# Dilated attention on one core: the product of the probabilities with V, its two exact halves in one matmul and its two heads in two banks

## The chip, the cores and the metric

The kernel runs on one core of a Trainium2 chip, as one launch. The metric is the device time of an execution in microseconds (us). TensorE (PE in the profile) multiplies matrices and writes to PSUM, which has eight banks of 512 float32 columns in each of 128 partitions. PEld is TensorE's loading of weights, which overlaps its matmuls. VectorE (DVE), ScalarE (ACT) and GpSimd (POOL) work beside it. DMAs are issued here from the queue of SyncE (SP) and of ScalarE.

## What is computed

A decoder trunk of two layers over 1024 positions of width 1024. The first layer mixes positions by a gated MLP, the second by attention; each is followed by a dense MLP with squared ReLU. The change lies in the attention. It has 8 heads of width 64 and three groups, each with its own queries, keys and values: dilations 1, 4 and 16, with windows of 128, 512 and 2048 positions. In each, a query attends to up to 129 keys, one dilation apart. Cut to what matters:

```python
def _dilated_group(q, k, v, bias_table, window, dilation):
    ...
    s = jnp.einsum('bnqrhc,bnkrhc->bnrhqk', qb, kc) * (HEAD_DIM ** -0.5)
    ...
    logits = jnp.where(valid[None, :, None, None], s + bias[None, None, None], NEG_INF)
    m = jnp.max(logits, axis=-1)
    p = jnp.exp(logits - m[..., None])
    den = jnp.sum(p, axis=-1)
    num = jnp.einsum('bnrhqk,bnkrhc->bnqrhc', p, vc)
    ...

def _dilated_attention_mixer(h, w_qkv, w_out, rel_bias):
    ...
    m_all = jnp.max(jnp.stack(maxs), axis=0)
    scales = [jnp.exp(m_ - m_all) for m_ in maxs]
    num_sum = sum(n_ * c[..., None] for n_, c in zip(nums, scales))
    den_sum = sum(d_ * c for d_, c in zip(dens, scales))
    o = (num_sum / den_sum[..., None]).astype(h.dtype).reshape(B_, S_, ATT_WIDTH)
    return o @ w_out
```

The line that the change touches is `num`, the product of the probabilities p with the values.

## The kernel before

Everything is kept transposed: channels on partitions, positions along the free axis. Products are made with more than one pass: `split` (lines 207 to 209) writes a float32 array as a rounded half `hi` (ScalarE's copy, L208) and the rest `lo` (VectorE's subtraction, L209). A dense product is three matmuls, hi by hi, hi by lo and lo by hi.

The attention is worked in 12 units: four pairs of heads (`hp`), and for each pair the three groups in the order dilation 4, 16, 1 (`ORDER`, `g` = 1, 2, 0). A unit has four blocks `j` of 256 queries, in two parts of 128. A block passes through three steps:

- `scores` (L1086): twelve matmuls give the scores of both heads, in two banks; VectorE adds the bias and takes the row's extreme (L1105), ScalarE takes the exponential and its sum (L1107). The tiles of probabilities are called `t`.
- `turned` (L1111): TensorE transposes each head's probabilities in blocks of 128 by 128 (L187, two to four blocks a head), and `split` makes the halves `ph` and `pl`, tiles `tr` (in the last unit `p`), with one instruction on ScalarE (L208) and one on VectorE (L209) for each head.
- `values` (L1124): V lies in SBUF as hi and lo of both heads side by side, so that a stationary block of 128 columns is hi and lo of one head. Each block of keys is multiplied with `ph` and then with `pl` into the same columns of one bank `pv`, which holds both heads (256 queries each). A block of keys that both parts of the queries see takes 256 columns, others 128. Then for each head ScalarE copies the product with V's lo half to `N` (L1144) and VectorE adds the product with V's hi half (L1145).

When all three groups of a pair are there, `merge` weights and adds their `N`, and `project` multiplies the result by the output matrix and adds it to the residual `h` (L306).

PSUM is shared out in two pools: three banks `mm` for the projections of q and k and of the output (`mm_bank`), five banks `at` for the attention's steps (`at_bank`). A tile gets a bank when an earlier one has been read out.

The order on TensorE is written by the planner `Flow`: the main stream multiplies q and k of the next unit (24 matmuls of 512 columns per half, 8 groups of three), and between those groups of three the generators of the attention are resumed when the planned time (`LAT`) of what they wait for has passed. The other engines' order is chosen by a scheduler; `tc.high_priority` puts a few steps ahead. Each engine works through its queue in order. At a unit's last block, `exchange` (L1216) sends the statistics through memory (`sc`, `ex`), on SP's queue, on which the loads of the next bias rows (`bvec`, L906 and L911) stand too; a bias tile is turned round by VectorE at L916.

## Time and profile before

| what | value |
|---|---|
| median of three runs | 2191.18 us (2187.42, 2191.18, 2191.38) |
| the profiled execution | 2188.09 us, span 2186.4 us |
| mean granted clock of TensorE in it | 0.995 |
| TensorE busy | 2142.4 us, 98% of the span |
| VectorE, ScalarE, GpSimd busy | 71%, 50%, 24% |
| stretch of the attention's blocks | about 1065 to 1520 us of the span |

A row of the timeline gives the start, the time that it covers, the engine, the line and operation, output and inputs (without buffer numbers), shape and count; in brackets stands the idle time before it and what ended it. A matmul's duration overlaps the next one's, so the pace of a run of matmuls is read from the starts. A row of a group has the count, then busy us and mean ns of one, then idle time before and what ended it. A row of the waits has who waited for whom: us in total, how often, the longest.

### The profile page before, as it was taken

The page shows a single profiled execution, that of the slowest core. Times are in us where ns is not written, and L with a number is a line of the kernel's source. Part 1 is how long each engine was busy: PE and PEld are TensorE (multiplying, and loading weights), DVE is VectorE, ACT ScalarE, POOL GpSimd, SP SyncE. Part 2 cuts the span into 40 slices and gives each one's busy share as a digit, 9 for nine tenths or more (in the row PEclk, how much of TensorE's full clock was granted, in tenths as well). Part 3 has the DMA queues.
Part 4 walks back from the last instruction along what each step waited for, and adds up shares of the span by engine and source line. Part 5 has one row for each costly group of instructions (what it writes and reads, how often), then busy time and mean ns, then how long its engine had stood idle before and what let it go on. Part 6 is the DMA issues. An engine that isn't in the chain of part 4 may idle for free.

```text
span 2186.4 us, 30394 instructions
## 1 busy us (share of the span) xinstructions
PE 2142.4 (98%) x10360; PEld 1776.8 (81%) x10360; DVE 1551.1 (71%) x2855; ACT 1087.4 (50%) x2200; POOL 515.5 (24%) x372
## 2 busy tenths in 40 slices
PE   8999999999999999999999999999999999999997
PEld 7888887888878888788888887887778888788886
DVE  7875268766689887771357676658986667988867
ACT  7644135555564444351355564656555556544433
POOL 2000124333323333510000000001443332332335
PEclk9999999999999999999999999999999999999999
DMA  6321104444355443333322222221154443644422
GB/s 222 110 75 49 48 22 150 165 150 152 132 172 172 151 155 117 109 113 138 121 68 62 74 65 54 75 55 30 39 179 157 149 152 121 195 161 150 150 90 99
DMA packets 167679, 253.88 MB, mean 116 GB/s; under 512 B 33641, under 2 KB 59364, under 8 KB 167524
## 3 DMA queue, kind: packets, MB, share of 16 engines
q1 hardware_dynamic: 166768, 250.71, 35.7%
q8 instruction: 81, 1.33, 0.3%
q10 hardware_dynamic: 756, 1.23, 0.2%
q14 instruction: 74, 0.61, 0.1%
HBM read 182.50 MB, written 69.37 MB: 115 GB/s over the span
## 4 chain that ended last, share of the span: by engine, by line
PE 77%; DVE 10%; DMA 6%; ACT 4%; issue 2%; POOL 1%; SPq 1%; DVEq 0%; ACTq 0%; POOLq 0%
PE at L180 38%; PE mm L180 37%; PE at L187 1%; DVE wp L209 1%; ACT t L1107 1%; DMA t<-bvec 1%; DMA h<-in_xT 1%; DMA t<-hid 1%; DMA t<-in_w_dl 1%; DVE y L209 1%; DMA sc<-st 1%; DVE h L797 1%; DVE N L1145 1%; DMA hr<-hid 1%; DVE hx L209 1%
## 5 line engine op out<-in xcount | busy, mean ns | idle before, releaser
L208 ACT ACTIVATE wp<-r 128x512 fp32r<-128x512 f32 (+2 forms) x404 | 240.6, 600 | 359.1 <-PE at L180 240.3
L180 PE MATMUL at<-hx,wp 128*128 128x512 f32 x1770 | 413.1, 389 | 3.7 <-DVE h L797 3.7
L180 PE MATMUL mm<-y,whi 128*128 128x512 f32 x1312 | 412.3, 395 | 0.0
L180 PEld LDWEIGHTS at<-hx,wp 128*128 128x128 f32 x1770 | 332.0, 188 | 73.8 <-DVE h L797 4.5
L209 DVE TENSOR_TENSOR wp<-r,wp 128x512 fp32r<-128x512 f32 (+2 forms) x404 | 319.9, 801 | 66.0 <-ACT wp L208 62.3
L180 PE MATMUL at<-t,wp 128*128 128x512 f32 x1344 | 313.9, 389 | 0.1
L180 PEld LDWEIGHTS at<-t,wp 128*128 128x128 f32 x1344 | 252.2, 188 | 52.8 <-DVE t L713 0.5
L262 POOL TENSOR_TENSOR t<-t 128x512 f32<-128x512 f32 (+1 forms) x66 | 82.8, 1255 | 866.2 <-ACT t L257 864.1
L180 PEld LDWEIGHTS mm<-y,whi 128*128 128x128 f32 x1312 | 240.7, 188 | 50.6
L180 PE MATMUL mm<-y,wlo 128*128 128x512 f32 x656 | 255.9, 390 | 0.0
L180 PE MATMUL mm<-y,wp 128*128 128x512 f32 x912 | 224.3, 392 | 5.3 <-ACT t L694 4.8
L349 POOL TENSOR_TENSOR t<-r 128x512 f32<-128x512 f32 (+3 forms) x62 | 90.4, 1457 | 579.4 <-DMA r<-in_w_dn 164.2
L180 PEld LDWEIGHTS mm<-y,wp 128*128 128x128 f32 x912 | 171.5, 189 | 43.4 <-ACT t L694 5.7
L180 PE MATMUL mm<-hx,wp 128*128 128x512 f32 x708 | 172.4, 390 | 2.5 <-DVE hx L209 1.3
L180 PEld LDWEIGHTS mm<-hx,wp 128*128 128x128 f32 x708 | 132.6, 188 | 31.5 <-DVE hx L209 2.3
L209 DVE TENSOR_TENSOR hx<-t,hx 128x512 fp32r<-128x512 f32 x192 | 146.6, 770 | 1.8 <-ACT hx L208 1.8
L180 PEld LDWEIGHTS mm<-y,wlo 128*128 128x128 f32 x656 | 123.1, 188 | 26.6
L797 DVE TENSOR_TENSOR h<-h,at 128x512 f32<-128x512 f32 x144 | 97.6, 682 | 48.2 <-PE at L180 46.4
L209 DVE TENSOR_TENSOR wlo<-r,whi 128x512 fp32r<-128x512 f32 x138 | 97.6, 725 | 46.4 <-ACT whi L208 42.0
L208 ACT ACTIVATE hx<-t 128x512 fp32r<-128x512 f32 x192 | 119.0, 630 | 18.1 <-DMA t<-hid 11.7
L208 ACT ACTIVATE whi<-r 128x512 fp32r<-128x512 f32 x138 | 84.0, 627 | 88.3 <-PE mm L180 56.9
L180 PE MATMUL at<-y,wp 128*128 128x512 f32 x480 | 119.0, 390 | 0.7 <-DVE wp L209 0.7
(199 smaller groups left out, 3214.0 us busy)
## 6 DMA issues: line engine op xcount, KB each, us to landing
t<-hid SPq DMA_DIRECT2D x182, 256.0 KB, 3.5
hid<-t SPq DMA_DIRECT2D x140, 256.0 KB, 2.3
r<-in_w_up SPq DMA_DIRECT2D x128, 256.0 KB, 2.7
r<-in_w_dn SPq DMA_DIRECT2D x88, 256.0 KB, 2.6
hid<-b SPq DMA_DIRECT2D x56, 256.0 KB, 2.1
r<-in_w_qkv SPq DMA_DIRECT2D x50, 256.0 KB, 2.6
r<-in_w_v SPq DMA_DIRECT2D x48, 256.0 KB, 3.5
vd<-vs SPq DMA_DIRECT2D x16, 512.0 KB, 3.9
```

Of the source, the lines that this page charges most:

```text
L180: nc.tensor.matmul(out, lhsT, rhs, **kw)
L187: nc.tensor.transpose(out, src, ident)
L208: nc.scalar.activation(hi, src, AF.Copy)
L209: nc.vector.tensor_tensor(lo, src, hi.bitcast(F32), op=ALU.subtract)
L262: nc.gpsimd.tensor_tensor(self.acc, self.acc, sq, op=ALU.add)
L349: tt(r3, r[0, 0], r[1, 0], op=ALU.subtract)
L797: engine.tensor_tensor(hs[i, s], hs[i, s], src, op=ALU.add)
L1107: nc.scalar.activation(p[:, c], p[:, c], AF.Exp, bias=m, scale=-1.0, accum_out=dn)
L1145: nc.vector.tensor_tensor(o, o, pv[r, c], op=ALU.add)
```

## The change

`turned` splits the probabilities so that the halves of a part of the queries lie in one tile, hi first, lo behind: a tile [128, 2, columns] for each part and head, instead of one tile for each half. The number of tiles stays; for a head there are now two instructions on ScalarE and two on VectorE instead of one and one, each over that part's columns. In the last unit one tile still takes both parts, and one `split` does it.

`values` multiplies a block of V with both halves at once: the moving operand is [128, 2, 128], and the product goes to [128, 2, 128] of the bank, hi's product in its first 256 columns and lo's in its last 256. So a head needs a bank of its own: head 0 takes one from `at`, head 1 one from `mm`. ScalarE copies V's lo product with the probabilities' hi half; VectorE adds the hi product, and then, with an instruction more, V's hi product with the probabilities' lo half. The product of the two lo halves, which the kernel before took in, is left out. The planner counts as many columns as before, so the places of the steps on TensorE stay.

```diff
     def turned(u, j, ps, last=False):
-        _, _, width = geometry(u.g, j)
+        keys, at, width = geometry(u.g, j)
         out = []
         for p in ps:
             pt = at_bank()
             for b in range(width // P):
                 transpose(pt[:, blk(b)], p[:, blk(b)])
-            ph, pl = pair("p").both() if last else (rtemp(), rtemp())
-            with tc.high_priority(offset=PRIO):
-                split(ph[:, :width], pl[:, :width], pt[:, :width])
-            out.append((ph, pl))
+            if last:
+                x = slot((P, 2, HALF), F32R, "p")
+                with tc.high_priority(offset=PRIO):
+                    split(x[:, 0, :width], x[:, 1, :width], pt[:, :width])
+                pp = [x[:, :, at[i]:at[i] + keys[i][1] * P] for i in range(2)]
+            else:
+                pp = []
+                for i in range(2):
+                    x, w = rtemp().rearrange("p (e k) -> p e k", e=2), keys[i][1] * P
+                    with tc.high_priority(offset=PRIO):
+                        split(x[:, 0, :w], x[:, 1, :w], pt[:, at[i]:at[i] + w])
+                    pp.append(x)
+            out.append(pp)
         return out
 
     def values(u, j, pts):
         keys, at, _ = geometry(u.g, j)
-
-        parts = {}
-        for i in range(2):
-            for x in range(keys[i][1]):
-                parts.setdefault(keys[i][0] + x, []).append((at[i] + x * P, i * P))
-        pv = at_bank()
         for hd in range(2):
-            lst = list(parts.items())
-            for n, (kb, cs) in enumerate(lst):
-                pc, oc, w = cs[0][0], hd * 2 * P + cs[0][1], len(cs) * P
-                tv, at_ = place(u.g, kb)
-                va = u.V[tv][:, at_, 2 * hd:2 * hd + 2, :]
-                for e in range(2):
-                    matmul(pv[:, oc:oc + w], va, pts[hd][e][:, pc:pc + w], start=(hd == 0 and n == 0 and e == 0),
-                           stop=(n == len(lst) - 1 and e == 1), skip_group_check=True)
-        for hd in range(2):
+
+            pv = mm_bank() if hd else at_bank()
+            p3 = pv.rearrange("p (e q) -> p e q", e=2)
+            for i in range(2):
+                for x in range(keys[i][1]):
+                    tv, at_ = place(u.g, keys[i][0] + x)
+                    matmul(p3[:, :, blk(i)], u.V[tv][:, at_, 2 * hd:2 * hd + 2, :], pts[hd][i][:, :, blk(x)],
+                           start=(i == 0 and x == 0), stop=(x == keys[i][1] - 1), skip_group_check=True)
             r, x = slice(64 * hd, 64 * hd + 64), slice(64 - 64 * hd, 128 - 64 * hd)
-            o, c = u.N[r, 2 * j * P:(2 * j + 2) * P], slice(hd * 2 * P, (hd + 1) * 2 * P)
-            nc.scalar.activation(o, pv[x, c], AF.Copy)
-            nc.vector.tensor_tensor(o, o, pv[r, c], op=ALU.add)
+            o = u.N[r, 2 * j * P:(2 * j + 2) * P]
+            nc.scalar.activation(o, p3[x, 0], AF.Copy)
+            nc.vector.tensor_tensor(o, o, p3[r, 0], op=ALU.add)
+            nc.vector.tensor_tensor(o, o, p3[r, 1], op=ALU.add)
```

On TensorE the change replaces the rows of each call of `values` and leaves the others where they were. This is the first call, block 0 of the first unit (dilation 4), between the products of the main stream and the next transposes (`at` and `mm` are the pool of the output's bank, `tr` the halves):

```order
 L180 MATMUL mm<-y,whi 128x512 x2
 L180 MATMUL mm<-y,wlo 128x512
-L180 MATMUL at<-tr,V 128x256 x2
-L180 MATMUL at<-tr,V 128x128 x2
-L180 MATMUL at<-tr,V 128x256 x2
-L180 MATMUL at<-tr,V 128x128 x2
+L180 MATMUL at<-tr,V 128x2x128 x3
+L180 MATMUL mm<-tr,V 128x2x128 x3
 L187 MATMUL at<-ident,t 128x128 x6
```

Eight matmuls into one bank have become three into a bank of `at` and three into a bank of `mm`.

On VectorE, this is the place in the second pair's unit of dilation 4 at which block 0's product is read out, while the first pair is projected. Before, `at_10810` is the bank of both heads and `mm_10766` holds a half of the next unit's k:

```order
L1145 TENSOR_TENSOR N_10809<-N_10809,at_10810 64x256
L1062 SCALAR_TENSOR_TENSOR k1_10941<-mm_10766,k0_10940 128x32x16
L209 TENSOR_TENSOR tr_10828<-at_10823,tr_10827 128x384
L209 TENSOR_TENSOR tr_10836<-at_10831,tr_10835 128x384
L1145 TENSOR_TENSOR N_10809<-N_10809,at_10810 64x256
L1105 ISA t_10853,st1_10570<-at_10839,b_10100 128x128
```

The same place after it, where `at_10860` holds head 0's product and `mm_10867` head 1's, and `mm_10816` is that half of k:

```order
L1147 TENSOR_TENSOR N_10859<-N_10859,at_10860 64x256
L1062 SCALAR_TENSOR_TENSOR k1_11001<-mm_10816,k0_11000 128x32x16
L209 TENSOR_TENSOR tr_10878<-at_10874,tr_10878 128x128
L1148 TENSOR_TENSOR N_10859<-N_10859,at_10860 64x256
L1147 TENSOR_TENSOR N_10859<-N_10859,mm_10867 64x256
L209 TENSOR_TENSOR tr_10881<-at_10874,tr_10881 128x256
L209 TENSOR_TENSOR tr_10888<-at_10884,tr_10888 128x128
L1148 TENSOR_TENSOR N_10859<-N_10859,mm_10867 64x256
L1105 ISA t_10908,st1_10616<-at_10894,b_10133 128x128
```

Between the reading of k and the first scores stand three subtractions and three adds where two and one stood; a fourth subtraction follows behind the first scores.

On TensorE again, this is where that unit's last block is multiplied, in front of the next unit's first projection. Before (`mm_10944` is the second half of k, `mm_11032` an output projection, `mm_11053` the next unit's q):

```order
L180 MATMUL mm_10944<-y_8580,wlo_10756 128x512
L180 MATMUL at_11013<-tr_10979,V_10595 128x256
L180 MATMUL at_11013<-tr_10980,V_10595 128x256
L180 MATMUL at_11013<-tr_10979,V_10596 128x128
L180 MATMUL at_11013<-tr_10980,V_10596 128x128
L180 MATMUL at_11013<-tr_10987,V_10595 128x256
L180 MATMUL at_11013<-tr_10988,V_10595 128x256
L180 MATMUL at_11013<-tr_10987,V_10596 128x128
L180 MATMUL at_11013<-tr_10988,V_10596 128x128
L180 MATMUL mm_11032<-o_10806,whi_10693 128x512 x2
L180 MATMUL mm_11032<-o_10806,wlo_10692 128x512
L180 MATMUL mm_11053<-y_8347,whi_11044 128x512 x2
```

After it, with `mm_11004`, `mm_11098` and `mm_11119` in their places:

```order
L180 MATMUL mm_11004<-y_8580,wlo_10806 128x512
L180 MATMUL at_11078<-tr_11040,V_10641 128x2x128
L180 MATMUL at_11078<-tr_11043,V_10641 128x2x128
L180 MATMUL at_11078<-tr_11043,V_10642 128x2x128
L180 MATMUL mm_11085<-tr_11050,V_10641 128x2x128
L180 MATMUL mm_11085<-tr_11053,V_10641 128x2x128
L180 MATMUL mm_11085<-tr_11053,V_10642 128x2x128
L180 MATMUL mm_11098<-o_10856,whi_10743 128x512 x2
L180 MATMUL mm_11098<-o_10856,wlo_10742 128x512
L180 MATMUL mm_11119<-y_8347,whi_11110 128x512 x2
```

Between the second half of k and the next q there were one `mm` tile, and are now two.

## The prediction

> **What bounds the kernel now.** I read the page first, then the busy time by stretches, the groups of instructions by shape, the waits of the attention stretch, and the timelines of TensorE and VectorE around single products.
>
> ```profile
> span 2186.4 us, 30394 instructions
> ...
> PE 2142.4 (98%) x10360; PEld 1776.8 (81%) x10360; DVE 1551.1 (71%) x2855; ACT 1087.4 (50%) x2200; POOL 515.5 (24%) x372
> ```
>
> ```profile
> core 0: us, PE busy (x) PEld busy (x) DVE busy (x) ACT busy (x) POOL busy (x), PEclk, DMA share, GB/s
> 1065.00:1520.00 455.00, 446.90 (x2698) 371.31 (x2698) 297.05 (x888) 258.88 (x726) 2.14 (x2) 1.00 0.23 64
> ...
> 1490.00:1525.00 35.00, 32.05 (x185) 27.11 (x186) 31.82 (x74) 22.23 (x53) 6.49 (x5) 0.95 0.09 31
> ```
>
> TensorE is busy 98% of the span, and 446.90 of the 455 us in which the attention runs, at a granted clock of 1.00. VectorE has 297.05 us there (65%). So a matmul less is worth its time, as long as nothing makes TensorE wait afterwards. Only in the last 35 us is VectorE as full as TensorE (31.82 of 35.00).
>
> **What the matmuls cost.** The change touches 48 calls of `values`: 16 each for the three dilations. In a timeline row, the time of a run of matmuls is the distance from its start to the next row's start.
>
> ```profile
> L180 PE MATMUL at<-tr,V 128*128 128x128 f32 x276 | 40.0, 260 | 0.0
> ...
> L180 PE MATMUL at<-tr,V 128*128 128x256 f32 x112 | 24.2, 298 | 0.0
> ```
>
> ```profile
> 1097.46 1.04 PE L180 MATMUL at<-tr,V 128*128 128x256 f32 x8
> 1098.33 0.84 PE L187 MATMUL at<-ident,t 128*128 128x128 f32 x6
> ...
> 1129.49 1.01 PE L180 MATMUL at<-tr,V 128*128 128x128 f32 x8
> 1130.34 0.62 PE L187 MATMUL at<-ident,t 128*128 128x128 f32 x4
> ...
> 1505.99 2.93 PE L180 MATMUL at<-p,V 128*128 128x128 f32 x24
> 1508.75 0.63 PE L187 MATMUL at<-ident,t 128*128 128x128 f32 x4
> ...
> 2162.68 3.48 PE L180 MATMUL mm<-xe,we 128*128 128x256 f32 x27
> ```
>
> Eight matmuls of dilation 4 (four of 256 columns, four of 128; the row prints one shape) take 0.87 us. Eight of dilation 16, all of 128 columns, take 0.85 us. So a matmul costs 0.11 us whether it streams 128 or 256 columns: the instruction sets the price, not the columns. Dilation 1 has eight in block 0 and twelve in the others; two calls of twelve take 2.76 us, 1.38 each. Before: 16 x 0.85 + 20 x 0.87 + 12 x 1.38 = 47.6 us.
>
> After, every matmul streams 2 x 128 columns: 4 in a call of dilation 16, 6 in one of dilation 4 and in block 0, 8 in the other blocks: 64 + 120 + 96 = 280, where there were 432. The trace has no such two-piece operand. Its nearest rows are 0.109 us (0.87 / 8) and the 27 contiguous matmuls of 256 columns in 3.48 us, 0.12 to 0.13 each. I take 0.12, the row in which every matmul has 256 columns: 33.6 us. The gain on TensorE is 14.0 us (17.1 at 0.109, 12.3 at 0.127): 0.15 us per call of dilation 4, 0.37 of dilation 16, 0.42 for a later block of dilation 1. No row excludes a dearer two-piece read; that end is a rival below.
>
> The row of 0.85 us speaks against one rule. The Trainium skill ("TensorE: Matmul & The Clock Gate", Back-to-back issue gap) gives an isolated matmul a gap that goes by its columns, 134 cycles at 128 and 262 at 256. By it the same number of columns (71,680 before and after) would cost the same time and the gain would be nothing. The same section says that a stream of weight loads and matmuls is paced by both, which is what the eight in 0.85 us show.
>
> **What is added beside TensorE.**
>
> ```profile
> L1145 DVE TENSOR_TENSOR N<-N,at 64x256 f32<-64x256 f32 x96 | 40.0, 417 | 52.4 <-ACT N L1144 51.1
> ...
> L1144 ACT ACTIVATE N<-at 64x256 f32<-64x256 f32 x96 | 36.2, 378 | 91.1 <-PE at L180 56.3 <-DVE N L1145 33.2
> ...
> L1105 DVE CUSTOM_DVE_ANT_0 t<-at,b 128x128 f32<-128x128 f32 x104 | 26.3, 287 | 2.0 <-PE at L180 1.2
> ...
> L209 DVE TENSOR_TENSOR tr<-at,tr 128x384 fp32r<-128x384 f32 x38 | 19.3, 549 | 1.9 <-ACT tr L208 1.3
> ...
> L209 DVE TENSOR_TENSOR tr<-at,tr 128x512 fp32r<-128x512 f32 x18 | 12.4, 687 | 1.0 <-ACT tr L208 0.7
> L209 DVE TENSOR_TENSOR tr<-at,tr 128x256 fp32r<-128x256 f32 x32 | 12.1, 417 | 0.3 <-ACT tr L208 0.3
> ```
>
> A second add for each head is 96 x 0.417 = 40 us of VectorE. The 88 subtractions of the halves (43.8 us together) become 176: 74 of 256 columns at 0.38 and 102 of 128 columns at 0.25, the price of the 128-column row of L1105: 54 us, 10 more. ScalarE gets 88 instructions more as well. VectorE goes from 297 to 347 us of 455, 76%: not the bound. What counts is who waits behind it at each place.
>
> ```profile
> DVE N L1145 <- ACT N L1144: 51.1, 30, 4.5
> ...
> ACT N L1144 <- DVE N L1145: 33.2, 20, 4.5
> DVE b L916 <- DMA t<-bvec: 26.2, 10, 4.6
> ...
> PE at L187 <- ACT t L1107: 2.3, 12, 0.3
> ```
>
> The two heads now share one bank, and ScalarE's copy for head 1 waits for VectorE's add for head 0 (20 waits, 33.2 us). With a bank each, this alternation goes: four adds in a row take about what two adds with ScalarE between them took, so I price the longer chain at nothing (0.3 us earlier to 0.5 us later at each place are its ends). If the cover fails, the exponentials come later, and TensorE already waits for them 12 times.
>
> **Where the gain is lost.** (a) At a unit's last block.
>
> ```profile
> 1110.69 4.30 DMA sc<-st
> 1115.49 4.93 DMA t<-bvec
> ```
>
> ```profile
> 1120.51 0.43 DVE L916 COPY b<-t 128x512 f32<-128x512 f32 x1 [3.20 <-DMA t<-bvec]
> ```
>
> ```profile
> 1123.35 1.18 PE L187 MATMUL at<-ident,t 128*128 128x128 f32 x4
> ```
>
> The statistics of block 3 go to memory (4.30 us), the bias load stands behind them on SP's queue (4.93), VectorE stands still for it (3.20), then come its scores, the exponentials, and the next unit's four transposes, which take 1.18 us where others take about 0.6. This chain starts at the scores of block 3 and has no matmul of the change in it, but TensorE runs two calls of `values` meanwhile. Where the chain ends last, their gain only becomes waiting. I take seven of the eleven changes of unit: three after dilation 4 (0.30 each), two after 16 (0.74), two after 1 (0.84): 4.1 us.
>
> (b) The new bank comes from the three `mm` banks. Where projections are put between the blocks, `mm` tiles follow each other within a microsecond.
>
> ```profile
> 1214.91 0.63 PE L180 MATMUL mm<-o,whi 128*128 128x512 f32 x2
> ...
> 1215.60 0.62 PE L180 MATMUL mm<-o,whi 128*128 128x512 f32 x2
> ...
> 1216.30 1.03 PE L180 MATMUL at<-tr,V 128*128 128x256 f32 x8
> ...
> 1219.31 0.95 PE L180 MATMUL at<-k,q 64*128 64x128 f32 x12
> ```
>
> ```profile
> 1214.15 1.16 DVE L1062 SCALAR_TENSOR_TENSOR k<-mm,k 128x512 fp32r<-128x512 f32 x1 [0.68 <-ACT k L1061]
> ...
> 1216.24 0.42 DVE L1145 TENSOR_TENSOR N<-N,at 64x256 f32<-64x256 f32 x1
> ...
> 1217.81 1.88 DVE L306 TENSOR_TENSOR h<-h,mm 128x512 f32<-128x512 f32 x3
> ```
>
> By the changed order, the third projection (1215.60) needs the bank of the product before it, which is read out at about 1216.7: 1.1 us late. It ends at 1217.4, head 0 of the next product at 1217.75. Head 1 needs the bank of the first projection, which VectorE reads behind the scores, from 1217.81 to 1218.5. So the product ends near 1218.9 and the six transposes near 1219.6; the scores stood at 1219.31. That is 0.3 to 0.6 us late, take 0.5, and 0.3 of gain with it: 0.8 us, and the order repeats the pattern for the next pair of heads: 1.6 us.
>
> (c) The next unit's first projection.
>
> ```profile
> 1231.71 0.63 PE L180 MATMUL mm<-y,whi 128*128 128x512 f32 x2
> ```
>
> ```profile
> 1232.90 0.43 DVE L916 COPY b<-t 128x512 f32<-128x512 f32 x1 [3.27 <-DMA t<-bvec]
> ...
> 1233.85 1.12 DVE L1062 SCALAR_TENSOR_TENSOR k<-mm,k 128x512 fp32r<-128x512 f32 x1
> ```
>
> Ahead of this matmul the order now has three `mm` tiles that are not read out: the second half of k, head 1 of the product, the last projection. The first of them to be read is k, by L1062, which stands behind the copy that waits for the DMA: until 1234.97. TensorE, and everything queued on it, stands for 3.3 us; with 0.3 of gain eaten: 3.6 us (none if k is read before the copy, 4 if the copy itself comes later).
>
> (d) The end.
>
> ```profile
> 1516.44 0.73 PE L180 MATMUL mm<-o,whi 128*128 128x512 f32 x2 [1.96 <-DVE h L306]
> ```
>
> Here TensorE already waits 1.96 us for VectorE, which is full. Eight more adds are 3.3 us, of which I let 0.9 go into VectorE's gaps: 2.4 us later, and the last unit's gain (0.15 + 3 x 0.42 = 1.4) is swallowed: 3.8 us.
>
> **The sum.** 14.0 - 4.1 - 1.6 - 3.6 - 3.8 = 0.9 us less: 2188.09 - 0.9 = 2187.2 us for an execution like the profiled one (span 2186.4, 1.7 around it). The three runs go from 2187.42 to 2191.38; their median, 2191.18, lies 3.1 above the profiled one. I add half of that: 2188.7, told as 2189 us. A measurement of this kernel can tell about 0.2% (4.4 us) from no change, so the forecast is no change.
>
> **Rivals.** *The waits are absorbed (faster).* For it: 33.2 and 51.1 us of alternation between ScalarE and VectorE go, so scores and exponentials may come earlier, and (a) and the wait in (d) shrink. The Trainium skill ("PSUM — Partial Sum Buffer", PSUM bank collisions) says that two engines may not touch one bank's same quadrant at once and must be ordered; by that rule it is the second bank that parts them, and the 20 waits of L1144 agree. Against it: (b) and (c) stay. Without (a) and the 2.4 us of (d) the gain is 0.9 + 4.1 + 2.4 = 7.4 us: 2182. Chance 0.30.
>
> *VectorE's queue is late (slower).* The 50 us more on VectorE fall between scores and exponentials. It decides as soon as the chain is later by over 0.3 us where TensorE already waits: 12 places x 0.5 us = 6 us, and one more stop like (c), 3.6. The gain of 0.9 becomes a loss of 8.7: 2198. For it: four adds and four subtractions now stand in VectorE's row where four instructions stood. Against it: 24% of VectorE is still free. Chance 0.22.
>
> *Columns, or the two-piece operand, set the price (slower).* TensorE then gains nothing, and the waits stay: 2 x 0.5 + 3.3 + 2.4 = 6.7 us more: 2196. This is what the skill's isolated gap would make of it; the 0.85 us speak against it. Chance 0.06. That the change doesn't do what it says is excluded by the order: 280 matmuls stand there.
>
> **How the numbers follow.** No change 0.42, faster 0.30, slower 0.22 + 0.06 = 0.28. The range reaches to both main rivals and takes in the half of 3.1 us that I can't place: 2180 to 2199; beyond it lie the full gain of 14 us (2176) and several stops like (c).
>
> **What would show it.** In the profile after: 280 matmuls `tr,V` and `p,V`, eight or six of them at 0.12 us each; a wait of TensorE on an `mm` tile for L1062 of 2 to 4 us near 1232, and for L306 near 1217 and 1332; unchanged times of the transposes after a unit's change; the wait before the last projections at 3 to 5 us. If TensorE's idle time in the attention stays near 8 us, I am wrong towards faster; if it grows by over 20, towards slower.

## The result, and the profile after

| | us |
|---|---|
| after, median of 4 runs | 2218.93 (2217.66 to 2222.29) |
| before, median of 4 runs beside them | 2190.66 (2187.42 to 2191.38) |
| ratio, 95% interval | 1.0135 (1.0122 to 1.0147) |
| forecast | 2189.0, range 2180 to 2199 |

The change makes the kernel 28.3 us slower. The forecast was no change, and the result lies outside its range. The page of the kernel after begins so:

```profile
span 2216.8 us, 30352 instructions
...
PE 2144.1 (97%) x10208; PEld 1766.9 (80%) x10208; DVE 1597.2 (72%) x3039; ACT 1100.6 (50%) x2288; POOL 517.7 (23%) x372
```

The stretch of the attention in the busy times by stretches (columns as in the prediction):

```profile
1065.00:1520.00 455.00, 425.29 (x2436) 343.72 (x2435) 317.25 (x1019) 256.53 (x784) 0.00 (x0) 0.98 0.23 62
```

TensorE is busy for 425.29 of these 455 us, where it was busy for 446.90. So its idle time in them went from 8 to 30 us, though it has fewer matmuls to do. The prediction had named a growth by over 20 us as the sign of its being wrong towards slower. The matmuls themselves did what was forecast. These are the groups of the new products by shape, and one call of dilation 16 in TensorE's timeline:

```profile
L180 PE MATMUL mm<-tr,V 128*128 128x256 f32 x125 | 23.7, 289 | 2.8 <-DVE h L306 1.8 <-DVE tr L209 1.0
...
L180 PE MATMUL at<-tr,V 128*128 128x256 f32 x125 | 21.9, 281 | 0.0
```

```profile
1131.35 0.40 PE L180 MATMUL at<-tr,V 128*128 128x256 f32 x2
1131.58 0.40 PE L180 MATMUL mm<-tr,V 128*128 128x256 f32 x2
1131.82 0.60 PE L187 MATMUL at<-ident,t 128*128 128x128 f32 x4
```

Four matmuls of 2 x 128 columns take 0.47 us from the first start to the next instruction, 0.12 each, where eight took 0.85. What is new is who waits. From the waits of the attention's stretch (1065 to 1560 us) after:

```profile
ACT t L1107 <- DVE st L1105: 86.0, 55, 9.4
ACT tr L208 <- DVE tr L209: 53.0, 79, 1.3
DVE b L916 <- DMA t<-bvec: 29.1, 10, 5.6
...
PE at L187 <- ACT t L1107: 12.4, 17, 2.1
...
PE mm L180 <- DVE h L306: 5.2, 7, 1.0
PE mm L180 <- DVE N L1148: 5.0, 5, 1.2
...
PE mm L180 <- DVE k L1062: 4.2, 1, 4.2
```

TensorE waits 12.4 us for the exponentials (2.3 before). ScalarE's exponentials wait 86.0 us for VectorE's statistics. Before, the row of the same view was:

```profile
ACT t L1107 <- DVE st L1105: 50.4, 43, 2.3
```

By itself this wait of ScalarE's is no measure of the loss: it is 82.0 us in e7_two_banks_alone below, which is as fast as the kernel before. What counts is whether TensorE waits behind it. The wait of ScalarE's split for VectorE's (`ACT tr L208 <- DVE tr L209`) wasn't there before at all: the two splits of a head read the same bank in turns, copy, subtraction, copy, subtraction, and ScalarE's next copy waits for VectorE 79 times.

The first change of unit shows how the lateness comes about. This is VectorE's timeline after; before, the same copy stands at 1120.51 (in the prediction).

```profile
1117.64 0.67 DVE L209 TENSOR_TENSOR wlo<-r,whi 128x512 fp32r<-128x512 f32 x1
1121.85 0.43 DVE L916 COPY b<-t 128x512 f32<-128x512 f32 x1 [3.54 <-DMA t<-bvec]
1122.19 0.41 DVE L1147 TENSOR_TENSOR N<-N,at 64x256 f32<-64x256 f32 x1
1122.63 0.42 DVE L1147 TENSOR_TENSOR N<-N,mm 64x256 f32<-64x256 f32 x1
1123.09 0.41 DVE L1148 TENSOR_TENSOR N<-N,at 64x256 f32<-64x256 f32 x1
1123.53 0.42 DVE L1148 TENSOR_TENSOR N<-N,mm 64x256 f32<-64x256 f32 x1
1123.99 0.29 DVE L1105 CUSTOM_DVE_ANT_0 t<-at,b 128x128 f32<-128x128 f32 x1
```

Before, the first of these scores stood here:

```profile
1122.16 0.29 DVE L1105 CUSTOM_DVE_ANT_0 t<-at,b 128x128 f32<-128x128 f32 x1
```

And this is TensorE's timeline after, at the transposes that need these scores:

```profile
1124.93 1.49 PE L187 MATMUL at<-ident,t 128*128 128x128 f32 x4 [0.89 <-ACT t L1107]
```

VectorE stands still for 3.54 us at the head of its queue, because the bias copy waits for its load. Behind it stand four adds, and behind these the next scores. The transposes come at 1124.93 instead of 1123.35, with a wait of 0.89 us that the kernel before did not have. The chain of waits says why the copy itself is 1.34 us later than before. Two of its pieces:

```profile
1112.47 4.68 DMA sc<-st
...
1117.65 4.18 DMA t<-bvec
```

Before, the statistics left at 1110.69 (quoted in the prediction). Their path through VectorE, from k (L1062) over the adds and splits to the last block's scores, is longer now, and the bias load stands behind them on SP's queue. So VectorE's added work is paid ahead of the two DMAs and once more behind them, and VectorE's idle time lies between, where nothing that is queued behind the copy can use it.

The stop that the prediction's (c) expected is there too. VectorE's row of the copy, and TensorE's rows after:

```profile
1240.96 0.43 DVE L916 COPY b<-t 128x512 f32<-128x512 f32 x1 [4.03 <-DMA t<-bvec]
```

```profile
1243.10 1.19 PE L180 MATMUL mm<-y,whi 128*128 128x512 f32 x2 [4.21 <-DVE k L1062]
...
1244.51 1.05 PE L180 MATMUL mm<-y,whi 128*128 128x512 f32 x2
...
1245.79 1.05 PE L180 MATMUL mm<-y,whi 128*128 128x512 f32 x2
...
1251.05 0.62 PE L180 MATMUL mm<-y,whi 128*128 128x512 f32 x2
...
1251.75 0.62 PE L180 MATMUL mm<-y,whi 128*128 128x512 f32 x2
```

After the stop of 4.21 us a group of three matmuls takes 1.28 us (1244.51 to 1245.79), and 0.70 from 1251 on.

### The profile page after: what moved, and what is told of

Read it like the earlier page. It is cut to its first block, busy times and chain, and to the rows that moved or that the text cites. A ratio compares the mean times of both kernels' runs of the same rounds, so it can differ in the third digit from the quotient of the medians.

```text
span 2216.8 us, 30352 instructions
## 1 busy us (share of the span) xinstructions
PE 2144.1 (97%) x10208; PEld 1766.9 (80%) x10208; DVE 1597.2 (72%) x3039; ACT 1100.6 (50%) x2288; POOL 517.7 (23%) x372
## 4 chain that ended last, share of the span: by engine, by line
PE 72%; DVE 13%; ACT 5%; DMA 5%; issue 3%; POOL 1%; SPq 0%; DVEq 0%; ACTq 0%; POOLq 0%
PE at L180 38%; PE mm L180 33%; DMA t<-bvec 2%; ACT t L1107 2%; DVE tr L209 1%; DVE wp L209 1%; DVE N L1148 1%; DVE N L1147 1%; DVE t L1105 1%; DMA sc<-st 1%; PE at L187 1%; DMA h<-in_xT 1%; DVE y L209 1%; DVE h L306 1%; DVE hx L209 1%
## 5 line engine op out<-in xcount | busy, mean ns | idle before, releaser
L208 ACT ACTIVATE wp<-r 128x512 fp32r<-128x512 f32 (+2 forms) x404 | 240.9, 600 | 370.2 <-PE at L180 248.2
L209 DVE TENSOR_TENSOR wp<-r,wp 128x512 fp32r<-128x512 f32 (+2 forms) x404 | 322.4, 807 | 66.2 <-ACT wp L208 62.7
L209 DVE TENSOR_TENSOR hx<-t,hx 128x512 fp32r<-128x512 f32 x192 | 140.9, 740 | 1.2 <-ACT hx L208 1.2
L1107 ACT ACTIVATE t<-t,st 128x128 f32<-128x128 f32 (+1 forms) x192 | 84.4, 441 | 86.1 <-DVE st L1105 86.0
L208 ACT ACTIVATE hx<-t 128x512 fp32r<-128x512 f32 x192 | 118.9, 630 | 13.2 <-DMA t<-hid 8.4
L209 DVE TENSOR_TENSOR wlo<-r,whi 128x512 fp32r<-128x512 f32 x138 | 97.5, 728 | 38.6 <-ACT whi L208 34.2
L208 ACT ACTIVATE whi<-r 128x512 fp32r<-128x512 f32 x138 | 83.6, 626 | 78.1 <-PE mm L180 48.2
```

Source lines behind the costliest of these rows:

```text
L208: nc.scalar.activation(hi, src, AF.Copy)
L209: nc.vector.tensor_tensor(lo, src, hi.bitcast(F32), op=ALU.subtract)
L1107: nc.scalar.activation(p[:, c], p[:, c], AF.Exp, bias=m, scale=-1.0, accum_out=dn)
```

## The experiments

Each kernel was run beside the kernel before on the same chip; differences are from the median of those runs. The later expectations sometimes take differences of medians that were measured at different times (9 us for the first experiment, 25 for the second adds), where the differences below give 7.0 and 23.4. The profile after left three theories: the two splits of a head that alternate (theory 1), head 1's bank among those of the projections (theory 2, later B and H), and VectorE's added time (theory 3, later A and V).

| kernel | median, us | minus before | ratio (95%) |
|---|---|---|---|
| e1_copies_first | 2210.05 | +21.3 | 1.0103 (1.0088 to 1.0118) |
| e2_at_bank | 2243.81 | +55.0 | 1.0255 (1.0240 to 1.0270) |
| e3_both | 2232.03 | +43.3 | 1.0203 (1.0181 to 1.0224) |
| e4_split_alone | 2200.32 | +11.5 | 1.0054 (1.0039 to 1.0069) |
| e5_no_second_add | 2193.76 | +4.9 | 1.0025 (1.0015 to 1.0035) |
| e6_one_split | 2221.98 | +33.1 | 1.0152 (1.0137 to 1.0167) |
| e6_pool_control | 2196.06 | +7.2 | 1.0040 (1.0025 to 1.0054) |
| e7_two_banks_alone | 2188.94 | +0.1 | 1.0001 (0.9991 to 1.0011) |
| e8_dilation16_only | 2189.47 | +1.9 | 1.0007 (0.9997 to 1.0016) |
| e9_add_in_sbuf | 2216.65 | +29.0 | 1.0134 (1.0119 to 1.0149) |
| e10_before_more_vector | 2222.94 | +35.3 | 1.0163 (1.0146 to 1.0180) |
| e11_add_on_gpsimd | 2203.13 | +15.5 | 1.0068 (1.0053 to 1.0083) |
| e12_after_bias_gpsimd | 2194.11 | +5.8 | 1.0031 (1.0021 to 1.0041) |
| e13_before_bias_gpsimd | 2184.06 | -4.2 | 0.9977 (0.9968 to 0.9987) |
| e15_dil16_bias_gpsimd | 2180.02 | -8.3 | 0.9961 (0.9947 to 0.9976) |
| e16_add_and_bias_gpsimd | 2187.91 | -0.4 | 1.0000 (0.9990 to 1.0010) |
| e17_fewer_steps | 2194.06 | +4.9 | 1.0024 (1.0014 to 1.0033) |
| e18_fewer_steps_gpsimd | 2178.60 | -10.5 | 0.9958 (0.9941 to 0.9974) |

Nine of these medians lie in none of the ranges that stood on record for them: e1, e2, e4, e6_one_split, e10 and e12, and, by 2.1 us or less, e5, e8 and e16.

### The alternation of the splits, and the bank of head 1

e1_copies_first: in `turned`, both of ScalarE's copies of a head come before VectorE's two subtractions.

```diff
-                    split(x[:, 0, :w], x[:, 1, :w], pt[:, at[i]:at[i] + w])
...
+                for i in range(2):
+                    nc.scalar.activation(pp[i][:, 0, :ws[i]], pt[:, at[i]:at[i] + ws[i]], AF.Copy)
+                for i in range(2):
+                    nc.vector.tensor_tensor(pp[i][:, 1, :ws[i]], ..., op=ALU.subtract)
```

> The changed kernel, but in turned ScalarE first makes both rounded halves of a head (two copies), and only then VectorE subtracts twice: the same instructions, without the alternation of ScalarE and VectorE on one bank. Theory 1 (the alternation of the two splits holds up ScalarE, and with it the exponentials): the 53 us of waits of ScalarE's split for VectorE's go, and 15 to 25 us of the 28 come back: 2194 to 2204 us. Theory 2 (head 1's product takes a bank of the three mm banks, and TensorE waits for their reading): almost nothing changes, 2214 to 2219 us. Theory 3 (the 96 added adds and 88 added subtractions on VectorE make the exponentials late): no change either, 2215 to 2219 us.

e2_at_bank takes head 1's bank from the other pool, and e3_both has both edits.

```diff
-            pv = mm_bank() if hd else at_bank()
+            pv = at_bank()
```

> The changed kernel, but head 1's product takes a bank of the at pool, as head 0's does; the mm banks serve the projections alone, as before. Theory 2: the wait of 4.2 us before the next unit's first projection near 1243 us, the half clock behind it and the waits of about 1 us each among the output projections go: 12 to 16 us come back, 2203 to 2207 us, if the five at banks bear it. Theory 1 and theory 3: 2214 to 2220 us.

> Both edits of the two runs before it. If theories 1 and 2 each hold for their part, the sum: 2176 to 2192 us, that is the before kernel's time or up to 14 us under it. If theory 3 holds, over 2205 us.

e4_split_alone is the kernel before with each split in two parts, into the same tiles:

```diff
-                split(ph[:, :width], pl[:, :width], pt[:, :width])
...
+            for c in ([slice(0, width)] if last else [slice(at[i], at[i] + keys[i][1] * P) for i in range(2)]):
...
+                    split(ph[:, c], pl[:, c], pt[:, c])
```

> The kernel before, with one part of the change alone: turned splits each head's probabilities in two parts (two copies and two subtractions in turn on one bank), into the same tiles as before; the products stay as they were. Theory 1: 15 to 25 us slower than before, 2205 to 2216 us. Theory 2: as before, 2189 to 2193 us. Theory 3: a few us for the 10 us of added VectorE time, 2191 to 2196 us.

Copies first gave 7.0 us back (28.3 to 21.3), and the split in two parts alone cost 11.5. So the alternation has a part in the loss, but less than theory 1 said; in the 11.5 are also the 88 more instructions on each of the two engines. The five `at` banks for both heads made it 26.7 us worse, and with copies first 22 worse: the cure for the projections' banks takes a bank that the scores and transposes need. From the waits of e2_at_bank:

```profile
PE at L180 <- ACT tr L208: 21.1, 12, 2.7
...
PE at L180 <- DVE tr L209: 6.2, 5, 1.5
...
PE at L180 <- DVE N L1148: 3.4, 6, 1.2
PE at L187 <- DVE N L1148: 3.3, 5, 1.3
```

The first row is the largest: twelve times the scores (`at<-k,q`) wait for ScalarE's part of a split. The other three come to 12.9 us. None of the four is among the main waits of the kernel after. In turn the waits for an `mm` bank that L1148 or k holds are gone, so the rows are no sum for the 26.7.

### The second add, the second bank, one split

e5_no_second_add leaves out L1148:

```diff
-            nc.vector.tensor_tensor(o, o, p3[r, 1], op=ALU.add)
```

> The kernel after, without the second of VectorE's two adds of a head, so that the product of V with the low halves of the probabilities is left out of the sums N. What is taken away is 96 VectorE instructions of about 0.45 us (43 us of VectorE's time) and a third reader of each bank. The split alone cost 11.5 us and the fewer matmuls give 14, so some 31 us of the 28 us loss are still without a cause. Theory A (VectorE's added adds): 15 to 25 us come back, 2195 to 2204. Theory B (the banks: a second bank in each call, of the same three that the projections use): the adds are some 0.5 us of each bank's time, at most 5 to 8 us come back, 2211 to 2214.

e6_one_split has one split for each head, into a tile of twice the size from the weights' pool; e6_pool_control is the kernel before with such tiles.

```diff
+                x = slot((P, 2, HALF), F32R, "p") if last else wpool.tile([P, 2, HALF], F32R, tag="w", name="tr")
...
                     split(x[:, 0, :width], x[:, 1, :width], pt[:, :width])
...
-                for i in range(2):
-                    x, w = rtemp().rearrange("p (e k) -> p e k", e=2), keys[i][1] * P
...
```

> The kernel after, with one split of a head's probabilities again in place of two: both halves lie in one tile of twice the size, which is taken from the weights' eight tiles, since the probabilities' tiles are half as large. So the two engines no longer alternate on the bank of the transposes, and nothing else is changed. If the costs add up, the 11.5 us of the split alone come back: 2205 to 2209. If the two splits also lengthen the other waits (interaction), more: 2195 to 2203. If only the alternation counted, as in the first experiment, 9 us: 2209 to 2211. The kernel in the same call that has the larger tiles alone says what the weights' tiles cost.

> The kernel before, with the probabilities' two halves in one tile of the weights' eight in place of two of the smaller tiles: the same instructions, other memory. It is the control of the run with one split. If the weights' tiles are not short, 2186 to 2191, as before; if the weights of the next projection come later by it, slower by 5 us or more, and the run with one split is to be read against this one.

e7_two_banks_alone is the kernel before, with head 1's product in an `mm` bank:

```diff
-        pv = at_bank()
         for hd in range(2):
+            pv = mm_bank() if hd else at_bank()
...
```

> The kernel before, with the product of head 1 in a bank of the projections' three in place of the second half of head 0's bank: the matmuls, the splits and the adds are those of before. Theory B (banks): the projections wait for the reads of head 1, 10 to 20 us slower, 2199 to 2209. Theory A (VectorE's adds): 0 to 4 us slower, 2188 to 2193.

The second adds cost 23.4 us (28.3 to 4.9). The second bank alone changes nothing that these runs can tell (+0.1), although TensorE's stop for k is there in it, and is its longest wait. That is a balance: TensorE's 2.3 us of waiting for the exponentials at the transposes are gone in it. From its waits:

```profile
PE mm L180 <- DVE k L1062: 2.7, 1, 2.7
```

The runs with one split tell nothing clear: the larger tiles alone cost 7.2 us, and in e6_one_split TensorE waits mostly for late weights, which share that pool:

```profile
PE mm L180 <- DVE wlo L209: 21.5, 11, 4.3
```

### VectorE's time, or the bank

e9_add_in_sbuf puts in the place of the kernel after's second add an instruction of the same size that reads `N` alone.

> The kernel after, with the second add of a head replaced by a VectorE instruction of the same size that reads N alone (the larger of N and N), so that the product of V with the low halves of the probabilities is left out of the sums. Without the second adds the time was 2193.8, with them 2218.9: they cost 25 us. Here VectorE has the same 96 instructions of about 0.42 us at the same places, but each bank is free after the first add. Theory V (VectorE's time: what is queued behind the add comes later): 2212 to 2220. Theory H (the bank is held one instruction longer, and the next projection or scores wait for it): 2193 to 2200. Half of each: 2203 to 2209.

```diff
-            nc.vector.tensor_tensor(o, o, p3[r, 1], op=ALU.add)
+            nc.vector.tensor_tensor(o, o, o, op=ALU.max)
```

e10_before_more_vector puts that instruction into the kernel before, behind each add.

> The kernel before, with one more VectorE instruction behind each of its 96 adds into N: the larger of N and N, of the same size, which changes nothing in N. TensorE's work, the splits and the banks are those of before; VectorE has 96 times 0.42 = 40 us more. Theory V alone: as much as the second adds cost in the kernel after, 15 to 25 us, 2204 to 2214. If the added time counts only where each split is in two parts or each call has two banks to free, because the kernel before has room for it: 0 to 6 us, 2188 to 2195.

```diff
             nc.vector.tensor_tensor(o, o, pv[r, c], op=ALU.add)
+            nc.vector.tensor_tensor(o, o, o, op=ALU.max)
```

In the groups of e9_add_in_sbuf by shape, the instruction that stands for the add has the add's length (407 to 425 ns for the other two):

```profile
L1148 DVE TENSOR_TENSOR N<-N 64x256 f32<-64x256 f32 x96 | 39.9, 416 | 1.9
```

The time is that of the kernel after (+29.0 against +28.3), although no bank is held by it. So it is VectorE's time that costs, not the bank. In the kernel before, the same 40 us cost 35.3, and they show as the same wait, of TensorE and of its loading of weights (2.3 and 7.3 us in the kernel before). From the waits of e10_before_more_vector:

```profile
PEld at L187 <- ACT t L1107: 25.3, 45, 2.4
...
PE at L187 <- ACT t L1107: 14.6, 27, 2.0
```

So 0.9 us is lost in the kernel before, and 0.6 in the kernel after, for each us that VectorE is given at this place, in a stretch in which it was idle for 158 of 455 us. Not all of it is waiting: a part is the lower clock behind TensorE's stops (last section). That is the point at which my reasoning from shares of busy time broke.

e11_add_on_gpsimd takes the second add off VectorE.

> The kernel after, with the second add taken off VectorE: ScalarE copies the product with the low halves out of the bank (96 more copies of about 0.38 us, 36 us), into the probabilities' tile that is no longer read, and GpSimd, which is idle in this stretch, adds it to N. VectorE has 40 us less, and the bank is free after two copies and one add. Theory V: near the run without the second add, 2194 to 2204, by what the copies cost on ScalarE. Theory H: the bank is held as long as in the kernel after, 2212 to 2220. If ScalarE, which has the exps, is now the one that is late: over 2220.

```diff
-            nc.vector.tensor_tensor(o, o, p3[r, 1], op=ALU.add)
+            t = pts[hd][1][r, 0, 0:2 * P]
+            nc.scalar.activation(t, p3[r, 1], AF.Copy)
+            nc.gpsimd.tensor_tensor(o, o, t.bitcast(F32), op=ALU.add)
```

This gave 12.7 of the 28.3 us back: 36 us of copies on ScalarE are cheaper than 40 us of adds on VectorE, but not free. The copy out of the bank is there because of a rule in the Trainium skill ("PSUM — Partial Sum Buffer", The four PSUM rules): GpSimd can't reach PSUM. No run here shows it.

e8_dilation16_only is the kernel before with the new form in a third of the units.

> The kernel before, with the new form of the product in the units of dilation 16 alone (16 calls of 48): both halves of a head's probabilities, 256 columns each, fit one of the small tiles, so each head keeps one split; head 1's product goes to a bank of the projections' three, and there are 32 second adds. Gain 16 calls of 0.37 us = 5.9. If the adds cost their share of the 25 us, a third, 8 us: 2190 to 2193. If at these calls, which have the narrowest scores and splits (128 columns for one query block), VectorE has room: 2182 to 2186, and then this is a version faster than both.

```diff
+            if u.g == 2:
+                x = rtemp().rearrange("p (e k) -> p e k", e=2)
+                ph, pl = x[:, 0], x[:, 1]
...
```

(with the new `values` for `u.g == 2`.) The new form at dilation 16 alone is no different from before (+1.9, ratio 0.9997 to 1.0016): 5.9 us of matmuls saved, and about as much lost again.

### The copy at the head of VectorE's queue

e12_after_bias_gpsimd, e13_before_bias_gpsimd, e15_dil16_bias_gpsimd and e16_add_and_bias_gpsimd, in this order, move the copy of the bias tiles to GpSimd.

> The kernel after, with the copy that lays out each unit's bias tile moved from VectorE to GpSimd, which is idle in this stretch. The copy waits for its load at the head of VectorE's queue: 29.1 us of waiting in 10 places in the kernel after, 26.2 in the kernel before, and all that is queued behind it waits too. Theory Q (VectorE's idle third can't be used, because it is spent at the head of its queue, most of it behind this copy): 10 to 20 us come back, 2199 to 2209. Theory S (the added time counts by its place, between the products and the next scores, whatever VectorE does elsewhere): 0 to 5 us, 2214 to 2219.

> The kernel before, with the copy of the bias tiles on GpSimd in place of VectorE. Its chain of waits has the load of the bias rows in it (4.9% of the stretch). Theory Q: the kernel before has the same stops, but TensorE is hardly late there, so the gain is small, 2 to 6 us: 2182 to 2186. Theory S: no change, 2186 to 2190. If GpSimd's copy comes later than VectorE's and the first scores of a unit wait for it: slower, over 2192.

> The kernel before, with the new form of the product in the units of dilation 16 alone, and the copy of the bias tiles on GpSimd. The new form at dilation 16 alone made no difference that the runs could tell (2189.5), though its matmuls are 5.9 us less: what the second adds took must have been about as much. Theory Q: with room in VectorE's queue the 5.9 us come through, 2179 to 2184, and this is faster than both kernels. Theory S: 2187 to 2190.

> The kernel after, with the second add on GpSimd (the run before this gave 2203.1) and the copy of the bias tiles on GpSimd too. Theory Q: the gains add up in part, 2190 to 2198. Theory S: the copy changes nothing, 2201 to 2205. If GpSimd's copy is queued behind adds that wait (GpSimd waited 490 us for ScalarE's copies in that run) and the first scores of a unit come late: over 2206.

All four have this edit, on the kernels after, before, e8_dilation16_only and e11_add_on_gpsimd:

```diff
-        nc.vector.tensor_copy(t[:, :, 0:w], bass.AP(...))
+        nc.gpsimd.tensor_copy(t[:, :, 0:w], bass.AP(...))
```

Copies of 0.3 to 0.4 us, ten of them in the stretch, moved off VectorE, give back 22.5 of the 28.3 us in the kernel after (28.3 to 5.8), and 4.2 in the kernel before. The move also takes some 4 us of work off VectorE, in both kernels alike. The cost of the change leaves that out: with the copy moved in both, it is 10.0 us (-4.2 to 5.8) where it was 28.3. So some 18 us of it belong to the copy's place at the head of the queue, and 10.0 us stay without it, beside the 14.0 that the matmuls save. At dilation 16 alone the new form now gains: -8.3, 4.0 us beyond the move itself. With the adds on GpSimd too (e16), the change costs 3.8 us against e13_before_bias_gpsimd. The first change of unit in e12_after_bias_gpsimd, on VectorE:

```profile
1116.32 0.69 DVE L209 TENSOR_TENSOR wlo<-r,whi 128x512 fp32r<-128x512 f32 x1
1116.91 0.43 DVE L1147 TENSOR_TENSOR N<-N,at 64x256 f32<-64x256 f32 x1
1117.41 0.42 DVE L1147 TENSOR_TENSOR N<-N,mm 64x256 f32<-64x256 f32 x1
1117.87 0.41 DVE L1148 TENSOR_TENSOR N<-N,at 64x256 f32<-64x256 f32 x1
1118.31 0.42 DVE L1148 TENSOR_TENSOR N<-N,mm 64x256 f32<-64x256 f32 x1
1118.77 0.29 DVE L1105 CUSTOM_DVE_ANT_0 t<-at,b 128x128 f32<-128x128 f32 x1
```

On GpSimd, and on TensorE, in the same kernel:

```profile
1120.14 0.62 POOL L916 COPY b<-t 128x512 f32<-128x512 f32 x1 [156.08 <-DMA t<-bvec]
```

```profile
1122.59 0.60 PE L187 MATMUL at<-ident,t 128*128 128x128 f32 x4
```

The four adds are as long as before the move, but they run at 1116.91, in the time in which VectorE stood still, and the next scores come at 1118.77 instead of 1123.99. The transposes wait for nothing. The copy comes at 1120.14, after these scores: they did not need it. It lays out the bias of a later unit (128x512, where the next unit, of dilation 16, has 128x256), and stood ahead of them in the queue by nothing but the order. Over the whole stretch the waits of e12_after_bias_gpsimd say the same:

```profile
ACT t L1107 <- DVE st L1105: 53.6, 51, 3.7
...
PE at L187 <- ACT t L1107: 2.5, 5, 0.8
...
PE mm L180 <- DVE k L1062: 1.3, 1, 1.3
```

The exponentials wait 53.6 us (86.0), the longest wait 3.7 (9.4), TensorE waits 2.5 us for them (12.4), and the stop of 4.2 for k is one of 1.3.

### A version faster than both

e17_fewer_steps, and e18_fewer_steps_gpsimd, which has the second add on GpSimd as well:

> The kernel after with the copy of the bias tiles on GpSimd (2194.1) and fewer steps between ScalarE and VectorE in the splits: one split of a head in the units of dilation 16, where both halves fit one tile, and elsewhere both of ScalarE's copies before VectorE's two subtractions. If the alternation costs as much as in the first experiment, which gave 9 us back: 2183 to 2188, faster than the kernel before by some 3 us. If it cost only because VectorE was late anyway, which the copy's move has mended: 2191 to 2196. The form at dilation 16 alone gave 2180.0 with the copy moved.

> The kernel of the run beside this one, with the second add on GpSimd as well. With two splits this gave 6 us (2194.1 to 2187.9). If it adds up: 2177 to 2182, as fast as the form at dilation 16 alone or faster. If with fewer steps VectorE is no longer late, ScalarE's added copies cost more than they save: 2186 to 2192.

```diff
+            elif u.g == 2:
+                x = rtemp().rearrange("p (e k) -> p e k", e=2)
...
+                    split(x[:, 0], x[:, 1], pt[:, :width])
+                pp = [x[:, :, blk(0)], x[:, :, blk(1)], x]
```

(elsewhere copies first, as in e1_copies_first; both with the bias copy on GpSimd, e18_fewer_steps_gpsimd with the add there as well.) Fewer steps in the splits gave nothing beside the move of the copy (+4.9 against +5.8). With the add on GpSimd too, they gave 10.1 us (-0.4 to -10.5), and this is the fastest kernel of the study beside e15_dil16_bias_gpsimd, whose interval overlaps with its own. Its stretch:

```profile
1065.00:1520.00 455.00, 442.47 (x2601) 365.19 (x2600) 309.37 (x947) 303.19 (x888) 85.89 (x113) 1.00 0.24 64
```

Against the kernel before with the copy moved (-4.2), the new product is worth 6.3 us in it, of the 14 that its matmuls save. Why the steps of the splits count with the adds on GpSimd and not with the adds on VectorE is open.

## Why the prediction was wrong, point by point

- **TensorE bounds the stretch: right as a reading, wrong in what I drew from it.** "VectorE goes from 297 to 347 us of 455, 76%: not the bound." The amount of work was right: over the whole span VectorE's busy time grew by 46.1 us (1551.1 to 1597.2) where I had 50. But the free part of VectorE was not free at the place that counted. About half of its idle time stood in front of the bias copy (26.2 us) and in front of adds that waited for ScalarE's copies of the product (51.1), and what is queued behind a waiting instruction could not move into it. The added 40 us cost 35.3 in the kernel before, and 23.4 in the kernel after.
- **The matmuls' gain of 14.0 us: right.** 0.47 us for four matmuls, 0.12 each, so the rival of the two-piece operand falls. By the rule of the Trainium skill's isolated gap ("TensorE: Matmul & The Clock Gate", Back-to-back issue gap) nothing would have been gained; the 0.47 against 0.85 us speak against it here once more. (The low end of my gain is 12.0 at 0.127, not 12.3; the sum doesn't use it.)
- **The step that failed: "so I price the longer chain at nothing (0.3 us earlier to 0.5 us later at each place are its ends)".** At the first change of unit, from the copy to the scores it takes 2.14 us (1121.85 to 1123.99) where it took 1.65 (1120.51 to 1122.16), so the place itself is at the end that I named. But I priced each place alone. The chain runs through VectorE from block to block, then through the statistics' and the bias's DMA, and through VectorE again; each delay is carried into the next, and TensorE had nothing to spare where it ends. That the copy in this chain makes most of the loss is shown: 28.3 us become 10.0 with it off VectorE in both kernels. The second adds measured 23.4 us and the split in two parts 11.5, where I had written nothing. Less the 14.0 of the matmuls that makes 20.9 of the 28.3 us. The other 7.4 I can't give to one cause; the prices were measured one at a time and need not add up.
- **The cover that I named was one for another bank.** I saw that the alternation in the product's bank goes (20 waits, 33.2 us), and it did. The Trainium skill's rule on engines in one bank ("PSUM — Partial Sum Buffer", PSUM bank collisions) agrees. But parting the heads, with the stop for k that it brings, is worth nothing in the kernel before (e7_two_banks_alone, +0.1). And I did not see that the split in two parts sets up the same alternation in the bank of the transposes, 79 waits and 53.0 us.
- **(a), the gain eaten at a unit's change (4.1 us): too mild.** I let the gain of the matmuls be lost there and nothing more, because I held that chain to be fixed in time ("has no matmul of the change in it"), and forecast unchanged times of the transposes there. They came 1.58 us later at the first change. I had the row of the copy (3.20 us) and the chain of its DMAs before me, and did not ask what is queued behind the copy.
- **(b), the `mm` bank near 1215 (1.6 us): right in kind, too small.** After, TensorE waits on such banks for L306 5.2 us in 7 places and for L1148 5.0 in 5.
- **(c), the next unit's first projection (3.6 us): the stop right, its price not shown.** 4.21 us, behind the copy and k, as described; the slower matmuls behind it were not in my sum. With the copy moved it is 1.3. But in e7_two_banks_alone a stop of 2.70 us at the same place leaves the kernel's time as it was.
- **(d), the end (3.8 us): only the kind can be told.** After, the last projections wait in several small pieces (for L1148, for the factors, for `h`) instead of 1.96 us at once.
- **The rival "VectorE's queue is late" was the right one**, at a chance of 0.22, and its price was far too low: 12 places of 0.5 us and one more stop made 2198. Its argument against ("24% of VectorE is still free") was the mistake of the whole.

## What to carry to other kernels

An engine's idle time is room only if the work that you add can run in it: look where it stands in the engine's queue, and what instruction it stands in front of. An instruction that waits for a DMA at the head of an in-order queue makes all that follows it as late as the DMA; if its result is needed only later, move it to an engine that has nothing behind it before you count on the free share. And price a chain that passes one engine several times as a whole, from where it starts to where TensorE waits, not place by place.

## What the runs showed of the hardware

TensorE's stop of 4.21 us had an after-effect that I had not counted. Mean granted clock by stretches of 5 us in the kernel after (the last three columns are clock, DMA share and GB/s):

```profile
1240.00:1245.00 5.00, 1.91 (x5) 1.55 (x6) 3.92 (x8) 1.39 (x3) 0.00 (x0) 0.72 0.22 60
1245.00:1250.00 5.00, 5.00 (x22) 3.76 (x22) 2.13 (x4) 0.00 (x0) 0.00 (x0) 0.60 0.50 157
1250.00:1255.00 5.00, 5.00 (x27) 4.11 (x26) 1.62 (x9) 2.25 (x9) 0.00 (x0) 1.00 0.00 0
```

From 1243 to 1249 a group of three took 1.28 us instead of 0.70: the 14 matmuls between 1243.10 and 1249.11 would take 3.3 us at 0.70 for three, and took 6.0. So the stop of 4.21 us cost some 2.7 us more behind it. The Trainium skill ("TensorE: Matmul & The Clock Gate", The HAM clock gate) says that the array falls to half its clock after at least one idle window of about 3.4 us and comes back after at least one busy one as long. The stop of 4.21 us agrees with the first, and a return after some 6 us, more than one such window, with the second.

But the clock also falls behind shorter stops. In stretches of half a us, the granted clock is 0.50 from 1160.2 to 1163.6 us in the kernel after, behind a stop of 2.06 us that ends at 1157.69, and from 1406.0 to 1409.4, behind one of 1.87 us that ends at 1403.71, though TensorE is at work by then. In the kernel before it is so from 1517.6 to 1521.0, behind the 1.96 us of (d). So an idle window of 3.4 us is not needed here; what decides it, these runs don't show. An estimate of the price is the time for which TensorE is busy, times what its granted clock lacks to 1, summed over these stretches from 1065 to 1600 us of the profiled execution: 6.4 us in the kernel after and 1.7 in the kernel before; 15.3 in e10_before_more_vector, 18.7 in e2_at_bank, 4.9 in e12_after_bias_gpsimd, 8.4 in e17_fewer_steps and 1.7 in e18_fewer_steps_gpsimd. So, by these executions, nearly 5 of the 28.3 us are not waiting but slower matmuls behind waits. This part is contained in the prices of the experiments and does not come on top of them.

An add of 64 x 256 took the same 0.42 us whether it read PSUM and SBUF (0.406 to 0.425) or SBUF alone (0.416).
